# One weight tile for the state and output products of a chunked recurrence

## The chip, the cores and the metric

The kernel runs on one core of one Trainium2 chip. The metric is the device time of one execution in microseconds (us). A core has five engines with one instruction queue each: PE (TensorE, matrix products), DVE (VectorE), ACT (ScalarE), POOL (GpSimd) and SP (SyncE, which here only issues DMAs). Each engine takes its own instructions in order. In the profile PE's weight loads stand apart, as PEld.

## The reference, cut to what matters

The program is a trunk of two layers on 512 tokens of width 1024. The change touches the RWKV-7 branch of each layer:

```python
def rwkv7_scan(r, w, k, v, a, b):                    # 8 heads of 64 channels, 512 tokens
    def step(state, inp):
        r_t, w_t, k_t, v_t, a_t, b_t = inp
        sa = einsum('bhvk,bhk->bhv', state, a_t)
        state = state * w_t[:, :, None, :] + sa[..., None] * b_t[:, :, None, :] + v_t[..., None] * k_t[:, :, None, :]
        return state, einsum('bhvk,bhk->bhv', state, r_t)
    ...
# in rwkv7_branch, y is the scan's result, one head of 64 channels at a time:
    mean = jnp.mean(y, axis=-1, keepdims=True)
    var = jnp.mean(jnp.square(y - mean), axis=-1, keepdims=True)
    y = (y - mean) * lax.rsqrt(var + RWKV_LNX_EPS)
    ...
# in reference, for each layer:
        y_a, v_first = rwkv7_branch(cols_a, ...)     # then y_a @ w_branch_a
        y_b = dsa_branch(cols_b, ...)                # attention, then y_b @ w_branch_b
        merged = sigmoid(gate_a) * (y_a @ w_branch_a[l]) + sigmoid(gate_b) * (y_b @ w_branch_b[l])
        x = x + merged @ w_out[l]
```

After this come an attention into 256 memory tokens and a feed-forward part (dense in layer 0, eight experts in layer 1), which the change does not touch.

## The kernel before

**The recurrence in chunks.** The 512 tokens are cut into 8 chunks of 64, and the 8 heads into two groups `g` of 4. Within a group `jj` (0, 1) counts the pairs of heads and `e` (0, 1) the head of a pair; head `e` = 0 lives on partitions 0 to 63 and `e` = 1 on 64 to 127. What does not depend on the running state is worked out for all chunks at once: `rwkv_prep` makes decayed copies of the inputs, `rwkv_mats` the products of a chunk's tokens with each other, `rwkv_inverse` the inverse of a triangular matrix. `rwkv_chain` then walks the chunks. There are two layers with two groups each, so four such chains in the program.

**Operands of a chain.** `AM` holds for each head and chunk 192 columns on 128 partitions: columns 0 to 63 are a temporary, 64 to 127 weights for the output, 128 to 191 weights for the next state. `UV` holds the 128 x 64 matrix of the chunk's corrections and values. `art` holds 64 x 64 weights that multiply the incoming state `TT`: plane 0 for the next state and plane 1 for the output.

**A step of a chain.** For each of its four heads, a chunk makes two products for the next state, `AM[..., 128:192]` with `UV` (L885, weights 128 x 64) and `art` plane 0 with `TT` (L891, 64 x 64), added up in one PSUM bank `pS`. One DVE instruction (L893, 128 x 128) scales the sum of all four heads by the decay `WC` and writes the next chunk's `TT`. Two more products per head make the output, `AM[..., 64:128]` with `UV` (L900) and `art` plane 1 with `TT` (L906), in the banks `py0` and `py1`. The first chunk has no incoming state and the last makes no next one, which leaves 112 products in a chain. After four chunks, a half of the chain, `rwkv_center` takes each head's mean from the two banks (L919 the sums, L922 the subtraction) and writes `yc` to SBUF; after all eight, `rwkv_gn` normalises both halves (ACT L931 squares, DVE L932 and L934), turns them with four 128 x 128 transposes each (L938) and adds them to what the later steps use; `rwkv_out` (L951) multiplies by a gate and writes the pieces `yah` and `yal` for the branch's projection.

All these operands are 32-bit floats (f32). Each matrix product on f32 shows as two records on PE and two on PEld in the trace; a transpose shows as one.

**What runs beside it.** The branch and gate projections go through `proj_feat` (L285: f16 products of 128 x 128 weights with 512 columns). Its weights come from `wtile`: SP's queue loads the f32 tile `raw`, ACT converts it to `whi` (L263), DVE (L268) or, for every fourth tile, POOL (L266) makes the remainder `wlo`. The attention branch (L529, L546, L553) leaves its result in a DRAM buffer `ybd` (store L559), from which `branches` reads it back as `yb` (L1064) for the projections that run beside the second chain of a layer.

**What sets the order.** The program is written as generators, one for each branch, which `layer` advances in the turns of a written string (`ORDER`, L1633). A scheduler then orders the instructions of each engine by its own simulated timeline, so the order on an engine is not that of the code. The mixing stage of a layer has 8 PSUM banks: three in the pool `sm` (every tile that the recurrence names `pA`, `pB`, `paT`, `pG`, `pH`, `pMQ`, `pS`, `py0`, `py1`, `pyT`, `pg` takes one of these in turn), two for the attention, two for projections (`pf`) and one for `po`. The second group's inputs `sa`, `sr` and `bkb` wait in DRAM while the first group's chain runs: `rwkv_prep` stores them through SP's queue, and the loop that follows the first chain loads them into `art` and `bkb` again.

Of the kernel before, what the change touches and what calls it, by code (L numbers as in the profile page):

```python
# [19 lines left out]
P = 128  # L20
# [34 lines left out]
class Kern:  # L55
# [506 lines left out]
    def rwkv(self, l, cx, sx, hh, hl, ya):  # L562
# [60 lines left out]
        spill = [(self.dp.tile([P, 2, 8, 64], F32, name=f"spa{jj}", tag=f"spa{jj}", bufs=1),  # L623
# [74 lines left out]
    def rwkv_tiles(self, gp):  # L698

        t = lambda n, *s: gp.tile([P, *s], F32, name=n)  # L700
        return dict(AM=t("AM", 4, 8, 192), UV=t("UV", 8, 2, 2, 64), TT=t("TT", 2, 8, 64), TN=t("TN", 2, 8, 32),
                    art=t("art", 2, 2, 8, 64))

    def rwkv_prep(self, j, tp, q, art, spill=None):
# [49 lines left out]
        pa = art[:, 0] if spill is None else tp.tile([P, 8, 64], F32, name="sa", tag="tA")  # L754
        nc.vector.scalar_tensor_tensor(pa, ch(kr), -1.0, W[:, :, 0:64], OP.mult, OP.mult)
        pr = art[:, 1] if spill is None else tp.tile([P, 8, 64], F32, name="sr", tag="tB")
        nc.vector.tensor_tensor(pr, ch(r), W[:, :, 1:65], OP.mult)
        if spill is not None:
            nc.sync.dma_start(spill[:, 0], pa)
            nc.sync.dma_start(spill[:, 1], pr)  # L760
# [20 lines left out]
    def rwkv_mats(self, g, jj, q, G, bkb):  # L781


        nc, c = self.nc, self.c
        AM, UV, art = G["AM"], G["UV"], G["art"][:, jj]
        Xs = [slice(0, 64), slice(64, 128)]
        rmask = c["rmask"][:, None, :].to_broadcast([P, 4, P])
        for c4 in range(2):
            pA = [self.sm("pA") for _ in range(2)]
            for ci in range(4):  # L790
                for e in range(2):
                    nc.tensor.matmul(pA[e][:, ci * P:(ci + 1) * P], lhsT=bkb[Xs[e], c4 * 4 + ci].rearrange("p a b -> p (a b)"),
                                     rhs=art[Xs[e], :, c4 * 4 + ci, :], start=True, stop=True)
            for e in range(2):
                nc.vector.tensor_tensor(AM[:, 2 * jj + e, c4 * 4:c4 * 4 + 4, 0:P], pA[e].rearrange("p (c t) -> p c t", c=4),
                                        rmask, OP.mult)
        for e in range(2):
# [4 lines left out]
            nc.scalar.copy(AM[:, 2 * jj + e, :, P:192], pB.rearrange("p (c t) -> p c t", c=8))  # L802
        pa = self.sm("paT")
        for cc in range(8):
            for X in Xs:
                nc.tensor.matmul(pa[X, cc * 64:(cc + 1) * 64], lhsT=art[X, 0, cc, :], rhs=self.ident[X, X], start=True, stop=True)
        self.halves(UV[:, :, jj], pa)

# [23 lines left out]
    def rwkv_chain(self, g, tp, q, G):  # L832
# [25 lines left out]
        id2 = self.c["id2"][:, None, :].to_broadcast([P, 4, 64])  # L858
        for c4 in range(2):
            for jj in range(2):  # L860
# [6 lines left out]
                p4 = pq.rearrange("p (c x t) -> p c x t", c=4, x=2)  # L867
                cs = slice(c4 * 4, c4 * 4 + 4)
                nc.vector.tensor_tensor(art[:, jj, 0, cs, :], p4[:, :, 1, :], id2, OP.add)
                nc.vector.tensor_tensor(art[:, jj, 1, cs, :], p4[:, :, 0, :], art[:, jj, 1, cs, :], OP.add)  # L870

        ps = self.sm("pS")
        ys = []
        for cc in range(8):
            tt, T = cc // 2, slice((cc % 2) * 64, (cc % 2) * 64 + 64)
            if cc % 4 == 0:
                py = [self.sm("py0"), self.sm("py1")]
                first = {}
                fs = {}
            for jj in range(2):  # L880
                for e in range(2):
                    h, X = 2 * jj + e, Xs[e]
                    if cc < 7:
                        po = ps[X, (cc % 4) * P + jj * 64:(cc % 4) * P + jj * 64 + 64]
                        m = mm(po, lhsT=AM[:, h, cc, P:192], rhs=UV[:, cc, jj, e, :], start=e not in fs, stop=cc == 0,  # L885
                               skip_group_check=True)
                        if e in fs:
                            self.order(m.ins, fs[e])
                        fs.setdefault(e, m.ins)
                        if cc:  # L890
                            mm(po, lhsT=art[X, jj, 0, cc, :], rhs=TT[X, jj, cc, :], start=False, stop=True, skip_group_check=True)  # L891
            if cc < 7:
                nc.vector.tensor_tensor(TT[:, :, cc + 1, :], ps[:, (cc % 4) * P:(cc % 4 + 1) * P].rearrange("p (j t) -> p j t", j=2),  # L893
                                        WC[:, :, cc:cc + 1].to_broadcast([P, 2, 64]), OP.mult)
            for jj in range(2):
                for e in range(2):
                    h, X = 2 * jj + e, Xs[e]
                    yo = py[e][T, (tt % 2) * P + jj * 64:(tt % 2) * P + jj * 64 + 64]
                    k = e, cc % 2
                    m = mm(yo, lhsT=AM[:, h, cc, 64:P], rhs=UV[:, cc, jj, e, :], start=k not in first, stop=cc == 0,  # L900
                           skip_group_check=True)
                    if k in first:
                        self.order(m.ins, first[k])
                    first.setdefault(k, m.ins)
                    if cc:
                        mm(yo, lhsT=art[X, jj, 1, cc, :], rhs=TT[X, jj, cc, :], start=False, stop=True, skip_group_check=True)  # L906
            if cc % 4 == 3:
                ys.append(self.rwkv_center(tp, py, "tA" if cc < 4 else "tB"))
        for hf in range(2):
            self.rwkv_gn(tp, ys[hf], q, g, hf)  # L910

    def rwkv_center(self, tp, py, tag):

        nc = self.nc
        mean = tp.tile([P, 2, 4], F32, name="mean", bufs=2)
        yc = tp.tile([P, 4, 2, 64], F32, name="yc", tag=tag)
        pe = [p[:, 0:256].rearrange("p (a d) -> p a d", a=4) for p in py]
        for e in range(2):
# [836 lines left out]
```

## Time and profile before

| | |
|---|---|
| time, median of 3 runs | 2184.46 us (2177.66 to 2187.46) |
| profiled execution, its own time | 2181.56 us |
| its span, first to last instruction | 2179.8 us |
| mean granted TensorE clock | 0.962 |
| PE busy | 2038.4 us (94%), 16712 records |
| PEld busy | 1317.0 us (60%) |
| DVE busy | 1368.0 us (63%), 2326 instructions |
| ACT busy | 987.9 us (45%), 1545 instructions |
| POOL busy | 325.7 us (15%), 338 instructions |
| DMA | 332.48 MB, mean 153 GB/s |
| first chain of layer 0, its chunks on PE | about 283 to 338 us |
| second chain of layer 0 | about 477 to 524 us |
| first chain of layer 1 | about 1299 to 1359 us |
| second chain of layer 1 | about 1495 to 1551 us |

Busy times of different engines overlap, so only an engine with nothing to wait for in a stretch says what bounds that stretch. A row of a timeline gives start and length in us, engine, line, operation, the tiles (out<-in), how much of the array the weights take (partitions x columns), the shape of the moving operand, its type and the number of records; in brackets stand idle time before it and what ended that. Records on PE overlap in their lengths, so the cost of a run of records is read from the start of the first to the start of what follows.

### The profile page before, as it was taken

How to read it: one execution, taken by the hardware profiler on the slowest of the kernel's cores; microseconds unless marked ns; L12 is line 12 of the kernel's file. 1: busy time of each engine (PE TensorE's matmuls, PEld its weight loads, DVE VectorE, ACT ScalarE, POOL GpSimd, SP SyncE). 2: the span in 40 equal slices, each digit the busy share in tenths (PEclk: the TensorE clock that was granted, in tenths of full speed). 3: DMA queues.
4: the chain of work that ended last, by engine and by line, in shares of the span. 5: the costliest groups of instructions: out<-in, count | busy, mean ns of one | idle time of the engine just before them, and what ended most of it. 6: DMA issues, size and time to landing. Idle time of an engine off the chain costs nothing. (4 is left out here: it accounts for less than half of the span.)

```text
span 2179.8 us, 40496 instructions
## 1 busy us (share of the span) xinstructions
PE 2038.4 (94%) x16712; PEld 1317.0 (60%) x16712; DVE 1368.0 (63%) x2326; ACT 987.9 (45%) x1545; POOL 325.7 (15%) x338
## 2 busy tenths in 40 slices
PE   8998899898998999999999989999799799999997
PEld 4664455464464544444583555535355599999996
DVE  6767975644665433322567995463554688888886
ACT  5533334441353333321443443442233378887883
POOL 2351500002010000000251340001200120000002
PEclk9998999999998999999999999999899899999998
DMA  7342324342542333333334222334151799999993
GB/s 223 101 101 75 111 61 114 78 150 60 191 150 67 104 100 104 104 99 102 116 82 106 84 85 73 96 89 144 55 178 35 251 354 383 360 355 345 343 344 132
DMA packets 339538, 332.48 MB, mean 153 GB/s; under 512 B 93697, under 2 KB 255617, under 8 KB 339346
## 3 DMA queue, kind: packets, MB, share of 16 engines
q1 hardware_dynamic: 328240, 306.03, 44.2%
q10 hardware_dynamic: 8482, 15.39, 2.1%
q0 software_dynamic: 2624, 8.40, 1.1%
q8 instruction: 133, 2.18, 0.4%
q14 instruction: 59, 0.48, 0.1%
HBM read 297.05 MB, written 32.72 MB: 151 GB/s over the span
## 5 line engine op out<-in xcount | busy, mean ns | idle before, releaser
L263 ACT ACTIVATE whi<-raw 128x1024 f16<-128x1024 f32 (+3 forms) x242 | 226.9, 939 | 501.6 <-PE pf L285 278.0
L268 DVE SCALAR_TENSOR_TENSOR wlo<-raw,whi 128x1024 f16<-128x1024 f32 (+3 forms) x208 | 233.3, 1123 | 215.0 <-ACT whi L263 202.0
L1510 DVE SCALAR_TENSOR_TENSOR ewlo<-eraw,ewhi 128x1024 f16<-128x1024 f32 x265 | 320.2, 1219 | 57.7 <-ACT ewhi L1509 56.8
L285 PEld LDWEIGHTS <-whi 128*128 128x128 f16 x1888 | 183.6, 99 | 245.9 <-issue 48.0
L1509 ACT ACTIVATE ewhi<-eraw 128x1024 f16<-128x1024 f32 x265 | 276.6, 1053 | 77.7 <-PE py L1569 34.1
L1524 PE MATMUL pe<-XT,ewhi 128*128 128x144 f16 x2816 | 206.1, 226 | 0.5 <-issue 0.5
L1524 PEld LDWEIGHTS <-ewhi 128*128 128x128 f16 x2816 | 183.2, 98 | 1.2 <-issue 0.6
L285 PE MATMUL pf<-hh,whi 128*128 128x512 f16 x448 | 172.4, 385 | 5.0 <-ACT qe L481 2.6
L285 PE MATMUL pf<-hl,whi 128*128 128x512 f16 x448 | 172.0, 384 | 0.0
L285 PEld LDWEIGHTS <-wlo 128*128 128x128 f16 x944 | 92.0, 99 | 116.5 <-issue 15.9
L285 PE MATMUL pf<-fh,whi 128*128 128x512 f16 x336 | 127.3, 379 | 0.0
L285 PE MATMUL pf<-fl,whi 128*128 128x512 f16 x336 | 127.3, 379 | 0.0
L266 POOL TENSOR_TENSOR wlo<-raw,whi 128x1024 f16<-128x1024 f32 (+3 forms) x34 | 60.3, 1772 | 410.8 <-ACT raw L265 262.9
L1524 PE MATMUL pe<-XT,ewlo 128*128 128x144 f16 x1408 | 116.8, 226 | 0.1
L285 PE MATMUL pf<-hh,wlo 128*128 128x512 f16 x448 | 112.7, 385 | 0.0
L1569 PE MATMUL py<-HT,ewhi 128*128 128x144 f16 x1408 | 103.9, 227 | 0.1
L164 POOL TENSOR_TENSOR rs<-rs,nrm_e 128x1 f32<-128x1 f32 x28 | 16.7, 596 | 520.1 <-DVE rs L163 520.1
L1524 PEld LDWEIGHTS <-ewlo 128*128 128x128 f16 x1408 | 94.1, 98 | 0.3 <-DVE ewlo L1510 0.3
L1569 PEld LDWEIGHTS <-ewhi 128*128 128x128 f16 x1408 | 92.5, 98 | 0.3 <-issue 0.2
L285 PE MATMUL pf<-fh,wlo 128*128 128x512 f16 x336 | 79.4, 379 | 0.0
L345 PE MATMUL ptok<-whi,hh 128*128 128x256 f16 (+1 forms) x320 | 75.8, 276 | 0.0
L345 PE MATMUL ptok<-whi,hl 128*128 128x256 f16 (+1 forms) x320 | 75.5, 276 | 0.0
(437 smaller groups left out, 3886.0 us busy)
## 6 DMA issues: line engine op xcount, KB each, us to landing
raw<-in_w_in_dram SPq DMA_DIRECT2D x76, 512.0 KB
eraw<-in_moe_wg_dram SPq DMA_DIRECT2D x16, 2048.0 KB
eraw<-in_moe_wu_dram SPq DMA_DIRECT2D x16, 2048.0 KB
eraw<-in_moe_wd_dram SPq DMA_DIRECT2D x16, 2048.0 KB
eraw<-in_moe_wg_dram SPq DMA_DIRECT2D x8, 1536.0 KB
eraw<-in_moe_wu_dram SPq DMA_DIRECT2D x8, 1536.0 KB
eraw<-in_moe_wd_dram SPq DMA_DIRECT2D x8, 1536.0 KB
raw<-in_ffn_wg_dram SPq DMA_DIRECT2D x22, 512.0 KB
```

Of the source, the lines that this page charges most:

```text
L164: nc.gpsimd.tensor_tensor(out, out, self.nrm_e[:, :n], OP.pow)
L263: nc.scalar.activation(hi, raw, AF.Copy, scale=SW)
L266: nc.gpsimd.tensor_tensor(lo, raw, hi, OP.subtract)
L268: nc.vector.scalar_tensor_tensor(lo, raw, SW, hi, OP.mult, OP.subtract)
L285: self.nc.tensor.matmul(p, lhsT=w[:, k, :], rhs=x[k], start=first, stop=last)
L345: mm(p, lhsT=x[:, k0 + k, ts], rhs=w[:, k, :], start=k0 == 0 and t % 2 == 0 and first, stop=k0 + kg == kt and last, skip_group_check=True)
L1509: nc.scalar.activation(r[0], w, AF.Copy, scale=SW)
L1510: nc.vector.scalar_tensor_tensor(r[1], w, SW, r[0], OP.mult, OP.subtract)
L1524: mm(p[:, i * n:(i + 1) * n], lhsT=w[:, k, :], rhs=XT[:, k, h, :], start=z == 0, stop=z == len(ms) - 1)
L1569: mm(ps[d], lhsT=w[:, i, d * P:(d + 1) * P], rhs=HT[:, k, h, :], start=k == 0 and w is wh and h == 0 and d % per == 0, stop=k == FT - 1 an ...
```

## The change

Per head and chunk the two products with `AM` become one, and so do the two with `art`. `AM[:, h, cc, 64:192]` (128 columns of weights) with `UV` and `art[X, jj, cc]` (64 partitions x 128 columns) with `TT` each fill 128 partitions of PSUM: 64 of them the next state, 64 the output. For the state to land on the partitions of its head (`Xs[e]`, where `TT` lives), the two halves of the columns stand in one order for `e` = 0 and in the other for `e` = 1; the output lands on the opposite partitions `Ys[e]`. The sums of a head parity `e` go to a bank of their own, `pSy`, for four chunks.

With this go:

- `art` and its copy in DRAM are laid out as [partition, jj, chunk, plane, 64] in place of [partition, jj, plane, chunk, 64]; the stores of `sa` and `sr` to DRAM go to runs of 64 floats.
- `rwkv_mats` puts the columns of `AM` in the order of the parity, then writes an identity into the state's plane of `art`, so that one addition per half and `jj` updates both planes: one ACT copy (64 x 512) of the output's plane on partitions 64 to 127, and two POOL copies (64 x 512) of `id2`.
- `TT` of the next chunk is written by two DVE instructions of 64 x 128, one per parity.
- The outputs of a chunk go from PSUM to `yc` in SBUF by two ACT copies of 64 x 128, and `rwkv_center` works in place on `yc` with instructions of 128 x 512.
- `yc` now holds a token's rows by parity on opposite partitions, so the turn before the gate is 16 f32 products of 64 x 64 with the identity per half in place of four 128 x 128 transposes.

```diff
@@ rwkv, rwkv_tiles, rwkv_prep @@
-        spill = [(self.dp.tile([P, 2, 8, 64], F32, name=f"spa{jj}", tag=f"spa{jj}", bufs=1),
+        spill = [(self.dp.tile([P, 8, 2, 64], F32, name=f"spa{jj}", tag=f"spa{jj}", bufs=1),
-                    art=t("art", 2, 2, 8, 64))
+                    art=t("art", 2, 8, 2, 64))
-            nc.sync.dma_start(spill[:, 0], pa)
-            nc.sync.dma_start(spill[:, 1], pr)
+            nc.sync.dma_start(spill[:, :, 0, :], pa)
+            nc.sync.dma_start(spill[:, :, 1, :], pr)
@@ rwkv_mats @@
-                nc.vector.tensor_tensor(AM[:, 2 * jj + e, c4 * 4:c4 * 4 + 4, 0:P], pA[e].rearrange("p (c t) -> p c t", c=4),
-                                        rmask, OP.mult)
+                am = AM[:, 2 * jj + e, c4 * 4:c4 * 4 + 4, :].rearrange("p c (x t) -> p c x t", x=3)
+                nc.vector.tensor_tensor(am[:, :, 0:3 - e:2 - e, :], pA[e].rearrange("p (c x t) -> p c x t", c=4, x=2), rmask, OP.mult)
...
-            nc.scalar.copy(AM[:, 2 * jj + e, :, P:192], pB.rearrange("p (c t) -> p c t", c=8))
+            nc.scalar.copy(AM[:, 2 * jj + e, :, 64 + 64 * e:P + 64 * e], pB.rearrange("p (c t) -> p c t", c=8))
...
         self.halves(UV[:, :, jj], pa)
+
+        id2 = c["id2"][:, None, :].to_broadcast([P, 8, 64])
+        nc.scalar.copy(art[Xs[1], :, 0, :], art[Xs[1], :, 1, :])
+        for e in range(2):
+            nc.gpsimd.tensor_copy(art[Xs[e], :, e, :], id2[Xs[e]])
@@ rwkv_chain @@
-                nc.vector.tensor_tensor(art[:, jj, 0, cs, :], p4[:, :, 1, :], id2, OP.add)
-                nc.vector.tensor_tensor(art[:, jj, 1, cs, :], p4[:, :, 0, :], art[:, jj, 1, cs, :], OP.add)
-        (per chunk: L885, L891, L893, L900, L906, as printed above)
+                at = art[:, jj, c4 * 4:c4 * 4 + 4]
+                nc.vector.tensor_tensor(at, pq.rearrange("p (c x t) -> p c x t", c=4, x=2), at, OP.add)
+        yc = []
+        for cc in range(8):
+            if cc % 4 == 0:
+                yc.append(tp.tile([P, 8, 64], F32, name="yc", tag="tA" if cc < 4 else "tB"))
+                p = [self.sm("pSy").rearrange("p (c j d) -> p c j d", c=4, j=2) for _ in range(2)]
+                first = [None, None]
+            for x in range(2 if cc else 1):
+                for e in range(2):
+                    for jj in range(2):
+                        if x:
+                            l, r = art[Xs[e], jj, cc].rearrange("p x t -> p (x t)"), TT[Xs[e], jj, cc, :]
+                        else:
+                            l, r = AM[:, 2 * jj + e, cc, 64:192], UV[:, cc, jj, e, :]
+                        m = mm(p[e][:, cc % 4, jj, :], lhsT=l, rhs=r, start=first[e] is None, stop=x == (1 if cc else 0),
+                               skip_group_check=True)
...
+            for e in range(2):
+                if cc < 7:
+                    X = Xs[e]
+                    nc.vector.tensor_tensor(TT[X, :, cc + 1, :], p[e][X, cc % 4], WC[X, :, cc:cc + 1].to_broadcast([64, 2, 64]), OP.mult)
+            for e in range(2):
+                nc.scalar.copy(yc[-1][Ys[e], 2 * (cc % 4):2 * (cc % 4) + 2, :], p[e][Ys[e], cc % 4])
             if cc % 4 == 3:
-                ys.append(self.rwkv_center(tp, py, "tA" if cc < 4 else "tB"))
+                self.rwkv_center(tp, yc[-1])
@@ rwkv_center, rwkv_gn @@
+        nc.vector.tensor_reduce(mean, yc, AX.X, OP.add)
         nc.vector.tensor_scalar(mean, mean, 1.0 / 64, None, OP.mult)
+        nc.vector.tensor_tensor(yc, yc, mean[:, :, None].to_broadcast([P, 8, 64]), OP.subtract)
...
         for jj in range(2):
-            for t in range(2):
-                nc.tensor.transpose(pt[:, (2 * jj + t) * P:(2 * jj + t + 1) * P], yc[:, 2 * t + jj].rearrange("p e d -> p (e d)"),
-                                    self.ident)
+            for ci in range(4):
+                for X, Y in zip(Xs, Xs[::-1]):
+                    nc.tensor.matmul(pt[X, (4 * jj + ci) * 64:(4 * jj + ci + 1) * 64], lhsT=yc[Y, 2 * ci + jj, :], rhs=self.ident[Y, Y],
+                                     start=True, stop=True)
```

In the changed file the products of a chunk are at L889, the update of `TT` at L897, the ACT copy of the outputs at L899, the turn `pyT` at L927.

Three places of the instruction order follow, before and with the change; the number of an instruction in its queue is left out, and a tile's number is part of its name.

PE, second chain of layer 1, one chunk between two projections, before (`pf` is a projection, `py_12575` and `py_12576` are the two output banks):

```order
L285 MATMUL pf<-yb,wlo 128x512
L885 MATMUL pS<-UV,AM 64x64
L891 MATMUL pS<-TT,art 64x64
L885 MATMUL pS<-UV,AM 64x64
L891 MATMUL pS<-TT,art 64x64
...
L906 MATMUL py_12575<-TT,art 64x64
L906 MATMUL py_12576<-TT,art 64x64
L900 MATMUL py_12575<-UV,AM 64x64
L906 MATMUL py_12575<-TT,art 64x64
L900 MATMUL py_12576<-UV,AM 64x64
```

The same place with the change, the whole chunk:

```order
L285 MATMUL pf<-yb,wlo 128x512
L889 MATMUL pSy<-UV,AM 128x64 x2
L889 MATMUL pSy<-TT,art 128x64 x2
L889 MATMUL pSy<-UV,AM 128x64 x2
L889 MATMUL pSy<-TT,art 128x64 x2
L285 LDWEIGHTS whi
L285 MATMUL pf<-yb,whi 128x512
```

Sixteen products that mostly alternate between a weight tile of 128 x 64 and one of 64 x 64 became eight that come in pairs of one shape. Over the whole PE queue, neighbouring products whose weights take another number of partitions or columns of the array (these two counts rounded up to 64 or 128) are 781 before and 514 with the change; of these, 390 and 105 lie within or at the edges of the chunks' products.

PE, second chain of layer 0, its beginning, before (`po<-pT,vt` is the attention's last product):

```order
L865 MATMUL pMQ<-AM 64x128 x16
L553 MATMUL po<-pT,vt 64x256 x4
L865 MATMUL pMQ<-AM 64x128 x16
L885 MATMUL pS<-UV,AM 64x64 x4
L900 MATMUL py_4159<-UV,AM 64x64 x3
L900 MATMUL py_4160<-UV,AM 64x64 x3
...
L900 MATMUL py_4160<-UV,AM 64x64
L285 LDWEIGHTS whi
L285 MATMUL pf<-yb,whi 128x512
```

And with the change:

```order
L553 MATMUL po<-pT,vt 64x256 x4
L285 LDWEIGHTS whi
L285 MATMUL pf<-yah_2773,whi 128x512
...
L861 MATMUL pH<-H_3996,TT 64x64 x8
L861 MATMUL pH<-H_3997,TT 64x64 x8
L870 MATMUL pMQ<-AM 64x128 x32
L889 MATMUL pSy<-UV,AM 128x64 x2
L285 LDWEIGHTS whi
L285 MATMUL pf<-yb,whi 128x512
```

The first projection that reads `yb` stood behind the first two chunks of the chain and now stands behind half of the first chunk; six projections of `yah` have moved in ahead of it.

ACT, second chain of layer 1, before (`whi<-raw` is the conversion of a weight tile for `proj_feat`):

```order
L200 CAST ybh<-po 128x256
L263 ACTIVATE whi<-raw 128x512 x3
L265 ACTIVATE raw<-raw 128x512
L263 ACTIVATE whi<-raw 128x512 x2
L931 ACTIVATE ysq<-yc 128x512
L263 ACTIVATE whi<-raw 128x256 x2
```

And with the change:

```order
L899 COPY yc<-pSy 64x128 x3
L263 ACTIVATE whi<-raw 128x512
L899 COPY yc<-pSy 64x128
L263 ACTIVATE whi<-raw 128x512
L899 COPY yc<-pSy 64x128
L265 ACTIVATE raw<-raw 128x512
L263 ACTIVATE whi<-raw 128x512
L899 COPY yc<-pSy 64x128 x2
L263 ACTIVATE whi<-raw 128x512
L918 ACTIVATE ysq<-yc 128x512
```

Between the conversions of the weights, ACT's queue now holds the copies of the chunks' outputs.

More of the change, by code (lines that the diff above doesn't have):

```diff
@@ L786, in rwkv_mats @@
         Xs = [slice(0, 64), slice(64, 128)]
-        rmask = c["rmask"][:, None, :].to_broadcast([P, 4, P])
+        rmask = c["rmask"].rearrange("p (x t) -> p x t", x=2)[:, None, :, :].to_broadcast([P, 4, 2, 64])
         for c4 in range(2):
@@ L805, in rwkv_mats @@
             for X in Xs:
-                nc.tensor.matmul(pa[X, cc * 64:(cc + 1) * 64], lhsT=art[X, 0, cc, :], rhs=self.ident[X, X], start=True, stop=True)
+                nc.tensor.matmul(pa[X, cc * 64:(cc + 1) * 64], lhsT=art[X, cc, 0, :], rhs=self.ident[X, X], start=True, stop=True)
         self.halves(UV[:, :, jj], pa)
+        id2 = c["id2"][:, None, :].to_broadcast([P, 8, 64])
+        nc.scalar.copy(art[Xs[1], :, 0, :], art[Xs[1], :, 1, :])
+        for e in range(2):
+            nc.gpsimd.tensor_copy(art[Xs[e], :, e, :], id2[Xs[e]])
     def rwkv_values(self, g, jj, q, G):
@@ L857, in rwkv_chain @@
             self.halves(UV[:, :, jj], ph)
-        id2 = self.c["id2"][:, None, :].to_broadcast([P, 4, 64])
         for c4 in range(2):
@@ L881, in rwkv_chain @@
                 for e in range(2):
[L882 to L885, printed above, removed]
-                               skip_group_check=True)
[L887 to L906, printed above, removed]
+                    for jj in range(2):
[4 more added lines that the diff above has]
+                        m = mm(p[e][:, cc % 4, jj, :], lhsT=l, rhs=r, start=first[e] is None, stop=x == (1 if cc else 0),
+                               skip_group_check=True)
+                        if first[e] is not None:
+                            self.order(m.ins, first[e])
+                        first[e] = first[e] or m.ins
@@ L909, in rwkv_chain, with rwkv_center @@
         for hf in range(2):
-            self.rwkv_gn(tp, ys[hf], q, g, hf)
-    def rwkv_center(self, tp, py, tag):
+            self.rwkv_gn(tp, yc[hf], q, g, hf)
+    def rwkv_center(self, tp, yc):
         nc = self.nc
[L915 to L918, printed above, removed]
-            nc.vector.tensor_reduce(mean[:, e, :], pe[e], AX.X, OP.add)
+        mean = tp.tile([P, 8], F32, name="mean", bufs=2)
+        nc.vector.tensor_reduce(mean, yc, AX.X, OP.add)
@@ L920, in rwkv_center @@
         nc.vector.tensor_scalar(mean, mean, 1.0 / 64, None, OP.mult)
-        for e in range(2):
-            nc.vector.tensor_tensor(yc[:, :, e, :], pe[e], mean[:, e, :, None].to_broadcast([P, 4, 64]), OP.subtract)
-        return yc
+        nc.vector.tensor_tensor(yc, yc, mean[:, :, None].to_broadcast([P, 8, 64]), OP.subtract)
     def rwkv_gn(self, tp, yc, q, g, hf):
```

21 lines of the change are left out of this document (6 added, 15 removed).

## The prediction

> **What bounds the kernel now.** I read the page's head first, then the busy times of each engine in stretches of 20 us around the four chains, then the timeline of PE inside one chunk.
>
> ```profile
> span 2179.8 us, 40496 instructions
> PE 2038.4 (94%) x16712; PEld 1317.0 (60%) x16712; DVE 1368.0 (63%) x2326; ACT 987.9 (45%) x1545; POOL 325.7 (15%) x338
> ```
>
> The second view gives for each stretch its length and the busy time (and instructions) of PE, PEld, DVE, ACT and POOL, then the granted clock, the DMA share and GB/s:
>
> ```profile
> 300.00:320.00 20.00, 20.00 (x123) 11.61 (x124) 13.73 (x41) 7.49 (x17) 3.78 (x2) 1.00 0.16 47
> 320.00:340.00 20.00, 20.00 (x130) 11.54 (x129) 11.96 (x30) 6.53 (x17) 0.00 (x0) 1.00 0.33 86
> 500.00:520.00 20.00, 20.00 (x139) 12.07 (x138) 5.76 (x12) 2.31 (x4) 8.34 (x6) 1.00 0.25 73
> 520.00:540.00 20.00, 13.45 (x54) 6.26 (x53) 11.07 (x22) 3.84 (x8) 4.47 (x4) 0.83 0.13 41
> 1520.00:1540.00 20.00, 20.00 (x136) 11.85 (x134) 9.18 (x18) 2.31 (x4) 8.63 (x6) 1.00 0.25 73
> 1540.00:1560.00 20.00, 12.53 (x76) 7.25 (x74) 6.24 (x17) 2.13 (x5) 5.28 (x7) 0.76 0.08 15
> ```
>
> Where the chains run, PE is busy 20.00 us of 20 while DVE has 6 us or more to spare and ACT 12 or more. PE sets the end there, and what is taken off it comes off the end, until a chain ends (the stretches from 520 and 1540, where PE waits for the normalisation). One chunk of a chain:
>
> ```profile
> 1536.54 0.33 PE L885 MATMUL pS<-UV,AM 128*64 128x64 f32 x2
> 1536.79 0.33 PE L891 MATMUL pS<-TT,art 64*64 64x64 f32 x2
> 1537.05 0.33 PE L885 MATMUL pS<-UV,AM 128*64 128x64 f32 x2
> ...
> 1538.45 0.33 PE L906 MATMUL py<-TT,art 64*64 64x64 f32 x3
> 1538.71 0.33 PE L900 MATMUL py<-UV,AM 128*64 128x64 f32 x2
> ...
> 1540.11 0.57 PE L285 MATMUL pf<-yb,whi 128*128 128x512 f16 x1
> ```
>
> From 1536.54 to 1540.11 are 3.57 us for 16 products (32 records). A product between two of the other shape takes 0.25 to 0.26 from start to start. Is that the array's time, or the price of alternating? Rows in which one shape repeats answer:
>
> ```profile
> 97.26 1.15 PE L806 MATMUL paT<-ct,art 64*64 64x64 f32 x32
> 98.34 0.69 PE L715 MATMUL pz<-x,wa 64*128 64x512 f32 x1
> ```
>
> Thirty-two records of 64 x 64 took 1.08 us, 0.034 each, so the two records of a product are worth 0.07 and **a change of shape costs 0.256 - 0.07 = 0.19 us**; with 0.054 a record (below) it is 0.15. I take 0.17. The chunk has 14 such changes, 2.4 us: two thirds of its time is alternation.
>
> **The change part by part.**
>
> *Removed: the chunks' products.* Their groups:
>
> ```profile
> L885 PE MATMUL pS<-UV,AM 128*64 128x64 f32 x224 | 33.2, 244 | 0.0
> L891 PE MATMUL pS<-TT,art 64*64 64x64 f32 x192 | 31.2, 242 | 0.0
> L900 PE MATMUL py<-UV,AM 128*64 128x64 f32 x256 | 34.7, 245 | 0.3 <-DVE art L870 0.3
> L906 PE MATMUL py<-TT,art 64*64 64x64 f32 x224 | 30.5, 241 | 0.0
> ```
>
> 896 records at the chunk's 3.57/32 = 0.112 would be 100 us. Summed chunk by chunk from start to next start, the four chains take 24.0, 23.9, 24.7 and 24.8 us: **97.4 us**; the first chunk of each chain is of one shape and cheaper.
>
> *Added: products of 128 columns.* 240 of them, 480 records. The nearest rows for what such a record costs are products with full 128 x 128 f32 weights, first with 2 columns streamed, then with 256:
>
> ```profile
> 646.41 0.95 PE L1176 MATMUL pss<-ones,aq 128*128 128x2 f32 x8
> 647.23 0.38 PE L285 MATMUL pf<-qh,wlo 128*128 128x512 f16 x1
> ...
> 681.76 1.03 PE L1189 MATMUL pms<-akT,aqT 128*128 128x256 f32 x4
> 682.62 0.81 PE L327 MATMUL ptok<-whi,oh 128*128 128x512 f16 x3
> ```
>
> With almost nothing to stream, eight records took 0.82 us: 0.102 each, which is then the weight load. With 256 columns four took 0.86: 0.215 each, or 0.054 for each 64 columns, with no room for a load on top. So the load runs behind the products, and a record with 128 weight columns and 64 streamed costs the larger of the two, 0.102, against 0.156 if the load stood in series. I take 0.102: 480 x 0.102 = 49.0 us. Shape changes at or within the chunks fall from 390 to 105: 105 x 0.17 = 17.9 (15.8 to 20.0). The new chains thus cost 66.9, **a gain of 30.5 us** (28 to 33 by the price of a change).
>
> Against this stands a rule of the Trainium skill, "TensorE: Matmul & The Clock Gate", Part 3 on packing small matmuls: a weight load overlaps running products only when it goes to other rows of the array. By it the full-height loads would run in series, 0.156 a record, and the gain would be 97.4 - 74.9 - 17.9 = 4.6 us. The 0.215 of L1189, whose weights fill all rows, does not agree with it here.
>
> *Other shape changes* in the PE order grow by 18 (514 - 105 against 781 - 390): +3.1 us.
>
> *The turn.* The transposes, in a warm and in a cold place:
>
> ```profile
> 523.76 0.66 PE L938 MATMUL pyT<-ct,yc 128*128 128x128 f32 x4
> 524.25 0.38 PE L285 MATMUL pf<-yb,whi 128*128 128x512 f16 x1
> ...
> 1558.99 1.09 PE L938 MATMUL pyT<-ct,yc 128*128 128x128 f32 x4 [7.47 <-DVE yc L934]
> 1559.87 3.62 PE L951 MATMUL pg<-x,g 128*128 128x512 f32 x4
> ```
>
> Eight halves at 0.49 are 3.9 us now; 256 records of 64 x 64 at 0.034 are 8.7: +4.8. Behind the wait at 1558.99 the same four transposes took 0.88, 1.8 times as long; there the 32 records should take 2.0, which is counted with the tail.
>
> PE alone: -30.5 + 3.1 + 4.8 = -22.6.
>
> *DVE and ACT.*
>
> ```profile
> L893 DVE TENSOR_TENSOR TT<-pS,WC 128x128 f32<-128x128 f32 x28 | 8.1, 290 | 42.8 <-PE pS L891 42.8
> L869 DVE TENSOR_TENSOR art<-pMQ,ct 128x256 f32<-128x256 f32 x16 | 6.7, 418 | 2.4 <-PE pMQ L865 2.0
> L919 DVE TENSOR_REDUCE mean<-py 128x4 f32<-128x256 f32 x16 | 6.7, 424 | 6.3 <-PE py L906 5.7
> L922 DVE TENSOR_TENSOR yc<-py,mean 128x256 f32<-128x256 f32 x16 | 6.0, 418 | 0.1
> L409 ACT ACTIVATE vt<-ptok 128x128 f32<-128x128 f32 x4 | 1.1, 274 | 0.0
> L744 POOL COPY rnx<-rn 128x512 f32<-128x512 f32 x8 | 7.2, 903 | 0.3
> ```
>
> The update of `TT` splits in two of as many columns (56 x 0.29, +8.1 us of DVE); `art` and the centring do the same columns in half the instructions, nothing or a little less. Hidden: DVE has 6 to 14 us free in each 20. A chunk's answer comes 0.29 later, behind projections; without that cover it is 28 x 0.29 = 8 us. ACT gets 64 copies near 0.27 (17.5 us, 12 of 20 free): hidden too if they don't block (rival below).
>
> *The tails.* After the last chunk centring is no longer 2 x 0.424 + 2 x 0.418 = 1.7 but two copies, then at most 0.85 + 0.84: +0.5 in each layer. The turn adds 1.1 cold in layer 1 and about 0.5 in layer 0 beyond its warm cost: +2 together.
>
> *`rwkv_mats`.* The identity fills are two POOL copies near 0.9 and an ACT copy of some 0.6 for each of eight calls; POOL works 3.8 us or less in the stretches from 300 and 320. They free `art` later for `pMQ`, long after. Zero, or all of them in the open 8 x 0.25 to 8 x 0.5 = 2 to 4; I take +2.
>
> *The store of `sa` and `sr` in short runs* goes through SP's queue:
>
> ```profile
> 255.31 0.34 SPq L760 DMA_DIRECT2D spa<-sr  x1
> ...
> L660 SPq DMA_DIRECT2D art<-spa x4: 332/382/425, 338.4 to 1359.3; - x4
> ```
>
> It is issued at 255 and read back from 338 on: 83 us of cover. Nothing, if the other loads of SP's queue don't notice 2048 more packets among 339538.
>
> *The read-back of `yb`.* The new order moves the first projection that reads it:
>
> ```profile
> 482.77 1.02 PE L285 MATMUL pf<-yb,whi 128*128 128x512 f16 x4 [0.36 <-DMA yb<-ybd]
> ...
> 1499.28 1.01 PE L285 MATMUL pf<-yb,whi 128*128 128x512 f16 x2 [2.90 <-DMA yb<-ybd]
> ```
>
> In layer 0 two chunks stood between the attention's last product and this reader; now there are six projections (1.3 us), the products of `pH` and `pMQ`, and half a chunk: about 2 to 2.5 us less cover, where 0.36 was already uncovered. +2. In layer 1 it waited anyway: 0.
>
> **Sum:** -22.6 + 2 (tails) + 2 (`rwkv_mats`) + 2 (`yb`) = -16.6 us against the profiled 2181.56, which is 2.9 below the median shown. 2165.0 from the one, 2167.9 from the other; I say **2165**.
>
> **The rivals.**
>
> *More is saved* (10%). Products of 64 rows from the two heads could run side by side, as the 0.034 of L806 suggests (below its 0.054 for streaming 64 columns): 224 records at 0.05 in place of 0.102 take another 11 us, and uncovered terms of 4 drop: about 2150. Against it: in the new order two products of one head stand together, on the same rows.
>
> *The supply takes half back* (16%). PE's projections now come sooner, and their weights must too. ACT shows the slack:
>
> ```profile
> 1521.52 0.63 ACT L263 ACTIVATE whi<-raw 128x512 f16<-128x512 f32 x1 [4.82 <-PE pf L285]
> ```
>
> It waits for PE to give back a buffer, so the supply is ahead in the second chains; in the first ones DVE, at 13.73 of 20, is nearer to a bound. If DVE's 8 us came out in the open: 2173.
>
> *The load is in series* (10%), for a reason that L1189 does not show: 480 x 0.156 + 17.9 = 92.8, so the chains gain only 4.6, and 3.1 + 4.8 + 6 are added: 2181.6 + 9.3 = 2191. This is what the skill's rule above comes to (the Trainium skill, the same page and part).
>
> *ACT's queue becomes the wait* (13%, the slower side). The copies `yc<-pSy` wait for a chunk's last product, and behind them in the queue stand the conversions of weights (0.63 each) that the projections between chunks need; before, nothing in ACT's queue there waited for the chain save `ysq`. A blocked conversion is late by itself and the remainder `wlo`, about 1.3 us for a chunk; 28 chunks make 36 us: 2181.6 - 16.6 + 36 = 2201. It decides for a loss from 13 such chunks. Against: the same 4.82 of waiting, more than a conversion and a copy, and up to three buffers of weights ahead.
>
> **Chances.** Forecast 51% (2155 to 2175 by itself), the rivals as given. Half a per cent, 11 us, is about what can be told from no change: faster is below 2173.5. The forecast gives nine tenths of its chance there, the first rival all, the supply half: 0.66. The same: the rest of these two, most of the series load, a little of ACT's queue: 0.21. Slower 0.13. The range leaves out the ends of both rivals: 2147 to 2189.
>
> **What would show it.** Right: a full chunk of eight products near 2.3 us on PE from start to start, records of L889 0.10 apart where a shape repeats; PE's busy time 20 us or so lower; PE still at 20.00 in the stretches of the chains, which end earlier; no idle time of PE before L285 put down to ACT's `whi`. Wrong: records of L889 near 0.16 apart; PE idle before L285 with ACT's L899 ahead of it; PE waiting for DVE's L897 between chunks; a wait for `yb` in layer 0 well above 2.4.

## The result, and the profile after

The changed kernel takes 2149.95 us (median of 4 runs, 2147.86 to 2151.00); the kernel before, on the same chip, 2181.06 (2174.54 to 2187.46). The ratio is 0.9847, with a 95% interval of 0.9811 to 0.9883: **about 31 to 33 us faster, twice the 16.6 that the prediction's sum gave.** The range held it; the size did not hold. Timed again on another occasion the ratio was 0.9864 (0.9818 to 0.9909).

The head of the page of the changed kernel's profiled execution (2149.16 us):

```profile
span 2147.3 us, 40225 instructions
PE 2006.6 (93%) x16520; PEld 1310.3 (61%) x16520; DVE 1379.4 (64%) x2322; ACT 1011.8 (47%) x1617; POOL 334.8 (16%) x354
```

PE's busy time fell by 31.8 us and the span by 32.5. The gain came off PE almost one for one, so PE was the bound in the main, as the prediction read it. The chains now run at about 299 to 346, 476 to 515, 1304 to 1353 and 1481 to 1518 us. Stretches in and around them, with the columns of the prediction's table:

```profile
300.00:320.00 20.00, 20.00 (x114) 12.74 (x112) 19.15 (x58) 10.98 (x29) 2.14 (x1) 1.00 0.25 72
320.00:340.00 20.00, 20.00 (x133) 12.87 (x131) 7.73 (x24) 8.95 (x24) 1.65 (x1) 1.00 0.24 64
500.00:520.00 20.00, 15.13 (x121) 10.77 (x118) 11.83 (x23) 4.59 (x13) 8.29 (x6) 0.91 0.21 66
1300.00:1320.00 20.00, 16.35 (x95) 10.60 (x95) 19.50 (x53) 4.79 (x14) 0.00 (x0) 0.83 0.03 9
1480.00:1500.00 20.00, 20.00 (x129) 13.34 (x124) 8.62 (x18) 5.13 (x13) 7.32 (x5) 1.00 0.65 210
1500.00:1520.00 20.00, 18.38 (x135) 12.36 (x133) 11.71 (x26) 4.90 (x14) 8.43 (x9) 0.99 0.21 54
```

In most of them PE is still full until a chain ends (515 and 1518 us). The beginnings of the two first chains are the exception: there DVE is nearly full now (19.15 and 19.50 of 20), and from 1300 to 1320 PE is no longer. Before the change that stretch was

```profile
1300.00:1320.00 20.00, 20.00 (x115) 10.79 (x113) 12.55 (x34) 4.90 (x12) 0.00 (x0) 0.83 0.15 41
```

and PE waited nowhere within the two first chains. With the change it waits at their beginnings for DVE's update of `art` and for ACT's copies:

```profile
299.16 0.66 PE L889 MATMUL pSy<-UV,AM 128*128 128x64 f32 x4 [2.40 <-DVE art L873]
...
1300.69 3.34 PE L870 MATMUL pMQ<-AM 64*64 64x128 f32 x32 [2.65 <-ACT UV L836]
...
1307.90 0.66 PE L889 MATMUL pSy<-UV,AM 128*128 128x64 f32 x4 [1.16 <-DVE art L873]
...
1314.32 0.66 PE L889 MATMUL pSy<-UV,AM 128*128 128x64 f32 x4 [1.49 <-ACT yc L899]
```

In the whole trace these waits come to 3.6 us for `art`, 2.7 for `UV` and 1.8 for `yc`; before, PE waited 0.3 for `art` at these products and nothing for the others.

A full chunk in the second chain of layer 1:

```profile
1496.43 0.55 PE L889 MATMUL pSy<-UV,AM 128*128 128x64 f32 x4
1496.92 0.66 PE L889 MATMUL pSy<-TT,art 64*128 64x64 f32 x4
1497.50 0.66 PE L889 MATMUL pSy<-UV,AM 128*128 128x64 f32 x4
1498.09 0.66 PE L889 MATMUL pSy<-TT,art 64*128 64x64 f32 x4
1498.68 1.90 PE L285 MATMUL pf<-yb,whi 128*128 128x512 f16 x8
```

From 1496.43 to 1498.68 are 2.25 us, where the old chunk took 3.57 and the prediction expected 2.3. Each pair of products (4 records) takes 0.58 to 0.59 behind a change of shape, and 0.49 behind a projection, whose weights have the same 128 x 128. Summed from start to next start, by the names of the tiles, the four chains take 62.2 us; the old ones come to 98.3 in this way (97.4 in the prediction's sum by lines). This sum is used for all kernels below.

Not every chunk has that order. In 8 of the 28 chunks with both kinds of product, all four products of TT with art stand together, two on partitions 0 to 63 and two on 64 to 127:

```profile
1339.64 1.00 PE L889 MATMUL pSy<-UV,AM 128*128 128x64 f32 x8
1340.57 0.67 PE L889 MATMUL pSy<-TT,art 64*128 64x64 f32 x8
1341.17 1.15 PE L927 MATMUL pyT<-ct,yc 64*64 64x64 f32 x32
```

Eight records then take 0.60, no more than four of one head (0.59).

The turn and the tails, and the read-back of `yb`, by the timeline and by the view of waits:

```profile
521.33 1.98 PE L927 MATMUL pyT<-ct,yc 64*64 64x64 f32 x32 [6.19 <-DVE yc L921]
523.23 3.57 PE L940 MATMUL pg<-x,g 128*128 128x512 f32 x4
...
1524.60 1.97 PE L927 MATMUL pyT<-ct,yc 64*64 64x64 f32 x32 [6.22 <-DVE yc L921]
1526.50 3.70 PE L940 MATMUL pg<-x,g 128*128 128x512 f32 x4
```

```profile
477.60 0.59 PE L285 MATMUL pf<-yb,whi 128*128 128x512 f16 x2 [0.87 <-DMA yb<-ybd]
...
480.54 1.67 PE L285 MATMUL pf<-yb,whi 128*128 128x512 f16 x7 [1.96 <-DMA yb<-ybd]
...
1478.30 0.59 PE L285 MATMUL pf<-yb,whi 128*128 128x512 f16 x2 [1.89 <-DMA yb<-ybd]
```

The 32 records of a half's turn (16 products) take 1.90 us behind a wait, against 0.88 for the four transposes; the wait ahead of them is 6.2 in both layers, where it was 5.8 and 7.5. `yb` is now waited for in layer 0, 0.87 + 1.96 where it was 0.36, and less in layer 1, 1.89 where the first wait alone was 2.90.

### The profile page after: what moved, and what is told of

It is laid out like the page before. It is cut to its first block, busy times and chain, and to the rows that moved or that the text cites. A ratio compares the mean times of both kernels' runs of the same rounds, so it can differ in the third digit from the quotient of the medians.

```text
span 2147.3 us, 40225 instructions
## 1 busy us (share of the span) xinstructions
PE 2006.6 (93%) x16520; PEld 1310.3 (61%) x16520; DVE 1379.4 (64%) x2322; ACT 1011.8 (47%) x1617; POOL 334.8 (16%) x354
## 2 busy tenths in 40 slices
DMA packets 346706, 332.47 MB, mean 155 GB/s; under 512 B 101889, under 2 KB 263809, under 8 KB 346514
## 4 chain that ended last, share of the span: by engine, by line
PE 70%; DVE 15%; DMA 5%; issue 3%; ACT 2%; SPq 2%; POOL 1%; another core or an unknown queue 0%; ACTq 0%; DVEq 0%; POOLq 0%
PE pf L285 20%; PE pe L1513 12%; PE ptok L327 10%; PE py L1558 6%; PE ptok L345 3%; PE pf L297 3%; PE pSy L889 3%; DVE iacc L514 2%; DVE m L513 2%; DVE wlo L268 2%; PE po L553 1%; PE psc L529 1%; PE pl L503 1%; DVE pr L988 1%; PE pA L793 1%
## 5 line engine op out<-in xcount | busy, mean ns | idle before, releaser
L285 PEld LDWEIGHTS <-wlo 128*128 128x128 f16 x944 | 92.9, 100 | 113.0 <-issue 12.4
```

Source lines behind the costliest of these rows:

```text
L285: self.nc.tensor.matmul(p, lhsT=w[:, k, :], rhs=x[k], start=first, stop=last)
```

## The experiments

The prediction's model has three prices: 0.034 us for a record with 64 columns of weights, 0.10 for one with 128, and 0.17 for a change of the weights' shape. If they are right, most of the gain has nothing to do with fusing products: it is the ordering that fusing brought along. The rival is that products cost their time in any order and the gain is their number, 448 to 240. The runs take the two apart. The table has each kernel's result; "chains" is PE's time in the chunks' products from start to next start without idle time, "changes" the changes of shape at or within them and in the whole PE order, "clock" the mean granted TensorE clock of the profiled execution, and "lost" is (1 - clock) x span.

| kernel | median us | ratio to before (95%) | products | changes | chains us | clock | lost us |
|---|---|---|---|---|---|---|---|
| before | 2181.06 | | 448 | 390 / 781 | 98.3 | 0.962 | 83 |
| changed | 2149.95 | 0.9847 (0.9811 to 0.9883) | 240 | 105 / 514 | 62.2 | 0.960 | 86 |
| changed, again | 2149.18 | 0.9864 (0.9818 to 0.9909) | 240 | 105 / 514 | 63.6 | 0.958 | 90 |
| 64 columns, grouped | 2099.61 | 0.9616 (0.9569 to 0.9662) | 448 | 118 / 506 | 45.7 | 0.967 | 69 |
| the same, outputs first | 2106.92 | 0.9669 (0.9623 to 0.9716) | 448 | 124 / 530 | 45.8 | 0.970 | 63 |
| changed, alternating | 2185.72 | 1.0025 (0.9998 to 1.0052) | 240 | 231 / 628 | 87.2 | 0.953 | 103 |
| only UV with AM fused | 2144.38 | 0.9848 (0.9805 to 0.9891) | 352 | 68 / 449 | 45.4 | 0.955 | 96 |
| changed, grouped | 2152.00 | 0.9832 (0.9793 to 0.9871) | 240 | 76 / 461 | 53.7 | 0.949 | 110 |
| the same, rows alternate | 2148.12 | 0.9840 (0.9800 to 0.9881) | 240 | 73 / 452 | 54.1 | 0.957 | 92 |
| all copies doubled | 2167.01 | 0.9919 (0.9890 to 0.9949) | 240 | 118 / 515 | 70.5 | 0.957 | 93 |
| fills doubled | 2152.30 | 0.9877 (0.9841 to 0.9914) | 240 | 127 / 531 | 71.9 | 0.963 | 79 |
| copies on DVE | 2149.34 | 0.9869 (0.9816 to 0.9921) | 240 | 118 / 514 | 67.1 | 0.961 | 84 |

**The changed kernel again.**

> The changed kernel once more, on the chip of the three runs beside it, as what they are compared with. Between 2148 and 2155 us, some 30 us below the kernel before.

2149.18 us. It is what the three runs after it are held against.

**The old products, in another order.** In the code nothing but the order within a chunk differs from the kernel before (the scheduler orders the rest anew around it); `self.order` ties one instruction behind another on PE.

```diff
-        (per head: state UV, state TT; then per head: output UV, output TT)
+            for x in range(2):                       # state, output
+                for jj in range(2):
+                    for e in range(2):
+                        m = mm(out(jj, e) if x else state(jj, Xs[e]), lhsT=AM[:, h, cc, 64:P] if x else AM[:, h, cc, P:192],
+                               rhs=UV[:, cc, jj, e, :], ...)
+                        uv.append(m.ins)
+            for x in range(2):                       # then all of TT with art
+                ...
+                        m = mm(..., lhsT=art[Xs[e], jj, x, cc, :], rhs=TT[Xs[e], jj, cc, :], ...)
+                        for w in uv:
+                            self.order(m.ins, w)
```

(In chunk 4, where the output banks change, state and output are two groups.)

> The kernel before with its 448 products of 64 weight columns left as they are, but ordered within a chunk: first all products of UV with AM (128x64), then all of TT with art (64x64). Shape changes at or within the chunks fall from 390 to 118. Theory (the price is the change of shape, 0.17 us each): the chunks cost 480 records x 0.048 + 416 x 0.034 + 118 x 0.17 = 57 us in place of 98, so the kernel gets as fast as the changed one or faster: about 2140, with no fused product in it. Rival (a product costs its 0.22 us of array time in any order, and only their number counts): no gain, within 5 us of the kernel before.

2099.61 us: 81 us below the kernel before and 50 below the changed one, with all 448 products and no fused one. The rival is dead. A chunk of it on PE:

```profile
1448.90 0.45 PE L905 MATMUL pS<-UV,AM 128*64 128x64 f32 x8
1449.28 0.38 PE L889 MATMUL pS<-TT,art 64*64 64x64 f32 x5
...
1449.56 0.40 PE L889 MATMUL py<-TT,art 64*64 64x64 f32 x7
1449.88 0.68 PE L905 MATMUL py<-UV,AM 128*64 128x64 f32 x8
1450.40 1.89 PE L553 MATMUL po<-pT,vt 128*64 128x256 f32 x8
```

Sixteen products, 32 records, in 1.50 us (1448.90 to 1450.40) where the old order took 3.57 and the fused products take 2.25. The eight products of TT with art (16 records) fit in 0.60, their change of shape included; the prediction's 0.034 a record was, if anything, too much. The chains come to 45.7 us, not the 57 expected: four products of UV with AM take 0.38, and I had priced their records at 0.048 by such a row of before, which held a change too, so that the sum counted those changes twice.

The kernel gained 74.8 us of span, the chains 52.6. Of the other 22, PE's idle time takes 12.6: the second chain of layer 1 ends while projections are left to cover its tail, and the wait before the turn falls from 13.3 us in all to 3.3. The rest, some 9 us, was not traced by itself; the clock's account below differs by 14.

**The fused products, alternating.**

```diff
-            for x in range(2 if cc else 1):
-                for e in range(2):
-                    for jj in range(2):
+            for e in range(2):
+                for jj in range(2):
+                    for x in range(2 if cc else 1):
+                        ...
+                        if last is not None: self.order(m.ins, last)
```

> The changed kernel with its 240 products forced to alternate, UV with AM then TT with art for each head: shape changes at or within the chunks go from 105 to 231. Theory (0.17 us for each change): +126 x 0.17 = 21 us, about 2170. Rival (the number of products and their 0.097 us for a record set the time): within 4 us of the changed kernel.

```profile
1522.16 0.33 PE L890 MATMUL pSy<-UV,AM 128*128 128x64 f32 x2
1522.42 0.43 PE L890 MATMUL pSy<-TT,art 64*128 64x64 f32 x2
1522.78 0.43 PE L890 MATMUL pSy<-UV,AM 128*128 128x64 f32 x2
1523.14 0.43 PE L890 MATMUL pSy<-TT,art 64*128 64x64 f32 x2
1523.51 0.39 PE L285 MATMUL pf<-yb,whi 128*128 128x512 f16 x1
```

2185.72 us: with 240 fused products in the wrong order the whole gain is gone. The first product, behind a projection of its own shape, takes 0.26; each that follows a change takes 0.36. Two records at 0.097 are 0.19, so the change costs 0.17, the prediction's price. By the chains (87.2 against 63.6 with 126 changes more) it is 0.19. The chains explain 24 of the 37 us; the clock's account is 13 higher, which would be the others (an estimate, (1 - clock) x span).

**One product fused, the other not.** UV with AM as in the change, TT with art as two products of 64 x 64 into the same bank, all of UV ahead of all of TT, the rows of the two heads alternating.

```diff
-                            l, r = art[Xs[e], jj, cc].rearrange("p x t -> p (x t)"), TT[Xs[e], jj, cc, :]
+            for x in range(2 if cc else 0):
+                for jj in range(2):
+                    for e in range(2):
+                        m = mm(p[e][(Xs, Ys)[x][e], cc % 4, jj, :], lhsT=art[Xs[e], jj, cc, (e + x) % 2, :],
+                               rhs=TT[Xs[e], jj, cc, :], start=False, stop=True, skip_group_check=True)
```

> The changed kernel with only the product of UV with AM fused (128 columns of weights); TT with art is split again in two products of 64x64, and within a chunk all of UV stand ahead of all of TT. Theory (records of 64x64 cost 0.034 each, those of 64x128 cost 0.097; a change of shape costs 0.17): 448 x 0.034 in place of 224 x 0.097 is -6.5, and 68 changes in place of 105 are -6.3, so 10 to 15 us below the changed kernel, about 2137. Rival (fewer products is what pays): 112 products more at 0.1 to 0.2 us, 11 to 22 us above the changed kernel.

```profile
1496.89 1.00 PE L887 MATMUL pSy<-UV,AM 128*128 128x64 f32 x8
1497.82 0.47 PE L896 MATMUL pSy<-TT,art 64*64 64x64 f32 x16
1498.23 0.39 PE L285 MATMUL pf<-yb,wlo 128*128 128x512 f16 x1
```

Eight products of 64 x 64 took 0.41 us, with the change back to 128 x 128 within it. The chains fell by 18 us to 45.4, more than expected, with 112 products more. The whole kernel came down by only 5 (2144.38 against 2149.18), which the spread of the runs (2140.37 to 2154.29) doesn't tell from nothing, and not by the 10 to 15 expected: PE's idle time grew by 13 us, 8 of them in the triangular inverse, and the granted clock was lower, 0.955. The rival, 11 to 22 us slower, did not happen.

**The fused products, grouped, in two orders of their rows.**

```diff
+                        if x and cc != 4:
+                            for w in uv: self.order(m.ins, w)      # TT behind all of UV
+                        elif not x:
+                            uv.append(m.ins)
```

and in the second of them `jj` outside and `e` inside, the products of TT of the second `jj` each tied behind the product before it.

> The changed kernel with its order alone altered: within a chunk all four products of UV with AM (128x128), then all four of TT with art (64x128), two of one head's rows and two of the other's. Shape changes at or within the chunks fall from 105 to 76, in the whole PE order from 514 to 461. Theory (a change of shape costs 0.19 us, the slope between the changed kernel and its alternating form): 53 x 0.19 = 10 us, about 2140, and the chunks near 58 us on PE in place of 63. Rival (all is in the count of products): within 3 us of 2150.

> As the run before it, but the four products of TT with art alternate between the rows of the two heads (0 to 63, 64 to 127). If products on different rows run side by side (the prediction's first rival, and the rule that a load overlaps products on other rows only), a record of these drops from 0.097 to about 0.05: 224 x 0.047 = 10 us less than the run before it, about 2130. If each record costs its load in any case, within 3 us of the run before it.

The first, then the second:

```profile
1501.28 1.00 PE L890 MATMUL pSy<-UV,AM 128*128 128x64 f32 x8
1502.21 0.67 PE L890 MATMUL pSy<-TT,art 64*128 64x64 f32 x8
1502.81 0.60 PE L285 MATMUL pf<-yb,whi 128*128 128x512 f16 x2
```

```profile
1499.41 1.00 PE L890 MATMUL pSy<-UV,AM 128*128 128x64 f32 x8
1500.35 0.66 PE L890 MATMUL pSy<-TT,art 64*128 64x64 f32 x8
1500.94 0.60 PE L285 MATMUL pf<-yb,wlo 128*128 128x512 f16 x2
```

Here stands a surprise. Eight records of TT with art take 0.60 us, as long as the four records of one head in the changed kernel (0.59). Two products on rows 0 to 63 and two on rows 64 to 127, next to each other, run side by side, in both orders of the code, as they do in 8 chunks of the changed kernel. So neither expectation for the second run was right as put: the overlap is real, and the first run had it already. The chains fell by 9.9 and 9.5 us, to 54 where 58 was expected, but the kernels did not follow: 2152.00 and 2148.12, no difference from 2149 that can be told. Their granted clock was 0.949 and 0.957.

**The copies.**

```diff
-                nc.scalar.copy(yc[-1][Ys[e], ...], p[e][Ys[e], cc % 4])
+                for _ in range(2):
+                    nc.scalar.copy(yc[-1][Ys[e], ...], p[e][Ys[e], cc % 4])
```

and the three fills of `art` in `rwkv_mats` likewise; then the fills alone; then, in place of that, `nc.vector.tensor_copy` for the copies of the outputs.

> The changed kernel with each added copy made twice: the 64 copies yc<-pSy on ACT (17 us of ACT), and the identity fills of art in rwkv_mats, 8 on ACT (5 us) and 16 on POOL (14 us). Theory (all of them lie beside PE): within 4 us of 2150, as the prediction's zero end has it. Rivals: the fills cost what the prediction took, +2 us, or up to 4; or ACT's queue is the wait, with 0.26 for each of 64 copies and the conversions behind them: +17 us or more.

> The changed kernel with only the identity fills of art in rwkv_mats made twice (8 ACT copies and 16 POOL copies more). Theory (they lie beside PE; what the run with all copies doubled lost came from the order that the scheduler built, above all from the waits for TN in the inverse): no instruction on PE waits for them, and the time is 2150 plus or minus 10, by what the new order happens to cover. Rival (the fills cost time themselves): +2 to +4 us with idle time of PE that names art on POOL or ACT.

> The changed kernel with the 64 copies of a chunk's outputs on DVE in place of ACT (17 us more on DVE, 17 less on ACT). If ACT's queue were a wait in the changed kernel, this would be 5 us or more faster and the conversions of weights would stand earlier. Theory (ACT has 12 of 20 us free there): within 10 us of 2150, without idle time of PE moving off ACT's whi; DVE's own work may push the scaling of the state later.

All doubled: 2167.01 us, 17 above the changed kernel, just what the rival of ACT's queue asked for. But the waits of PE say something else. The longest of that kernel's list and its wait for ACT's conversions, then the same two rows in the changed kernel's second trace (us in total, times, longest):

```profile
PE pY L1016 <- DMA TN<-scrN: 20.7, 11, 7.7
...
PE ptok L327 <- ACT whi L263: 4.7, 3, 1.9
```

```profile
PE pY L1013 <- DMA TN<-scrN: 4.2, 3, 2.5
PE ptok L327 <- ACT whi L263: 4.1, 3, 1.6
```

PE hardly waited longer for ACT's conversions (4.7 against 4.1). It waited 16 us more for the inverse's blocks to come back from DRAM, a round trip that other products on PE cover in the changed kernel's order; the scheduler, given other instructions, built an order that leaves it bare. Other waits fell, so that PE's idle time as a whole grew by 12.6, and the chains took 7 more, with 13 changes of shape more. That doubling the copies brought this on by way of the order, and not by holding something up, was not shown by itself. With the fills alone doubled the median is 2152.30, 2 to 3 us up, which the spread of the runs doesn't tell from nothing; no wait of PE there names `art` on POOL or ACT, as the rival asked. The copies moved from ACT to DVE change nothing that can be told (2149.34): PE then waits 2.6 us for them, where it waited 1.8 and 0 in the two traces of the changed kernel for ACT's. So the copies on ACT cost the changed kernel 1.8 us at most.

**The best order once more.** The grouped kernel with 64 columns, with the output's products of UV first (`for x in ((1, 0) if cc != 4 else (0, 1))`, and the state's tied behind them where a bank doesn't change).

> The grouped kernel with 64-column products once more with another order inside the group: the output's products of UV with AM ahead of the state's. 124 shape changes at or within the chunks in place of 118. Theory (grouping is what pays, not one lucky order): chunks within 3 us of the 46 that they took on PE, total 2090 to 2120. Rival (the grouped kernel's 2100 was half luck of the order): 2130 or more, with the chunks still near 46.

2106.92 us, chains 45.8. It is the grouping that pays, and not one lucky order. Its rival, 2130 or more, did not happen. PE's idle time is that of before here (130.3 us against 131.3), so of the 76 us by which its span is shorter, the chains explain 52.5 and idle time 1; the clock's account, 63 us against 83, would be most of the rest.

## Why the prediction was right or wrong

Term by term, the prediction against the two traces (2181.56 and 2149.16 us):

| term | predicted | measured |
|---|---|---|
| chunks' products | -30.5 | -36.1 (-34.7 in the second trace) |
| the turn | +4.8 | +5.6 |
| other PE work (other shape changes), what is left of the span | +3.1 | -0.8 |
| tails, `yb`, `rwkv_mats` (idle time of PE) | +6 | -1.2 |
| sum | -16.6 | -32.5 (the span) |

- **What bounds the kernel: right in the main.** What PE lost in busy time, the span lost. That DVE's work stays hidden was wrong at the beginnings of the two first chains, where PE now waits for `art`, `UV` and `yc`, 8.1 us in all (4.8 in the second trace); the prediction put this at nothing. Waits elsewhere fell by as much, so that it doesn't show in the sum.
- **The price of a change of shape, 0.17: right**, and measured apart: 0.17 by single products of the alternating kernel (0.14 with the 0.112 a record of the next point), 0.19 by its chains. The chunk at 2.3 us came out at 2.25. That most of the old chunk was alternation is shown by the old products in another order, 1.50 in place of 3.57.
- **The chunks' gain of 30.5 was 4 to 6 us too small**: the products took 62 to 64 us and not 66.9. Most of this is the side-by-side run of the two heads in the chunks whose TT products stand together: 8 chunks with eight records and 3 with six, some 4 us (an estimate: 38 records at 0.097 to 0.112). The price of a record was about right: four took 0.39 between two projections, 0.097 each, and 4, 8 and 12 records of UV with AM, each with the change behind them, took 0.48, 0.93 and 1.38, 0.112 for each further one, against 0.102. The load is hidden: had it stood in series, a pair would have taken 0.62 before any change of shape. So the rival of 0.156 a record falls. The Trainium skill's rule ("TensorE: Matmul & The Clock Gate", Part 3 on packing small matmuls), that a load overlaps only products on other rows, does not agree with the 0.097 to 0.112 of full-height weights; that products on other rows do overlap agrees with the 0.60 for eight records.
- **The step that failed is the sum of the small costs.** I took +3.1, +2, +2 and +2, all of one sign, for things that the profile did not show; together they came to about -2. That is 11 of the 16 us by which the sum was off; the chunks are the rest. The fills: no wait names them, and doubling them cost nothing that can be told. The other shape changes: not seen, PE's other work fell by 0.8. The tails: the cold turn, the one behind a wait, cost its 1.9 as predicted, but the waits ahead of the two turns fell from 13.3 to 12.4 in all. `yb`: +2.5 in layer 0, where +2 was predicted, and the reverse in layer 1, where I took 0, so that the total went from 5.1 to 4.7. Here some of these terms hid and some turned round; I let each one count, though the old order too had its share of bare waits (`psc` and `pb` waited 4.7 and 6.0 us for DVE, 0 and 1.7 with the change). Which edit took those away was not tried.
- **The rivals.** "More is saved" named the right time, 2150, and in part the right reason: products of two heads do run side by side, but in 11 chunks and not in all, which saved some 4 us and not 11; in most chunks a head's pair stands alone and takes 0.59. The small costs fell away by 11 us and not by 4. That the two misses add up to its 2150 is luck. The supply did not take half back, though DVE's 19.50 of 20 from 1300 us on is its sign. The copies in ACT's queue held PE up for 1.8 us at most.
- **Two slips that change nothing.** The chances for "faster" add up to 0.64 (nine tenths of 0.51, then 0.10 and 0.08), not 0.66. The short runs of `sa` and `sr` raised the packets from 339538 to 346706, by 7168 and not 2048; no wait of PE names them.
- **What I didn't ask.** My own prices said that two products of 64 columns on 64 rows (four records at 0.034) are cheaper than one of 128 (two at 0.10), and that 2.4 of 3.57 us were alternation. So the order was to be changed, not the products: that gives 81 us, 53 of them in the chains. Of the 18 us by which the changed kernel's chains (63.6) lie above those 45.7, 10 are its order (53.7 when grouped) and 8 the fused products; the turn costs 5.6 more.

## What to carry to other kernels

Before making small products larger, look at whether neighbours have the same shape of weights: here a change cost about 0.17 us, five records' worth at 0.034, and putting equal shapes together gained 81 us with the same products, 53 of them in these products' own time. A list of small costs that no row of the profile shows should not be added up with one sign: each is a bound, some are hidden, and a rebuilt order moves waits both ways. When an order is rebuilt, compare PE's time in the part that was changed, its idle time and its granted clock apart, for the whole time mixes the three.

## What was not expected of the hardware

Products with 64 x 64 weights were cheaper than the prediction's 0.034 a record: sixteen records in 0.41 us with a change within it, under 0.026 each. That is less than half of the 0.054 that streaming 64 columns takes by the prediction's L1189, so products on different quarters of the array run at the same time; with 0.17 taken off for the change it is 0.015, so more than three of the four at once (an estimate). Two products on different rows with 128 columns of weights did so too (0.60 for eight records, 0.59 for four).

The granted clock differs between orders of the same work. The view of cores, for the old products grouped and the fused products grouped:

```profile
core 0: 2105.0 us, clock 0.967
```

```profile
core 0: 2158.0 us, clock 0.949
```

If all of the span followed the clock, the same work at full clock would be some 69 us shorter in the first and 110 in the second (an estimate): 41 us between two kernels that differ by 8 us in their chains. Both profiled runs are the slowest of their kernel. Over the runs that were timed, the clock was 0.967 to 0.975 for the first, 0.948 to 0.958 for the second and 0.953 to 0.968 for the kernel before. With (1 - clock) x span taken off, the spans of all kernels in the table stand within 9 us of where the chains put them (the turn's 5.6 us not counted): against the kernel before, the grouped fused kernel is 49 us lower (chains -45), the one with only UV fused 52 (chains -53), the changed one 36 (chains -36), the grouped old products 61 (chains -53). That may be why 10 us less in the chains could be lost. The stretches below full clock lie mostly at or just behind idle time of PE (in the prediction's table of stretches, 0.83 and 0.76 where PE was busy 13.45 and 12.53 of 20), so an idle PE seems to be paid for twice. But not all do: before the change the clock was 0.83 from 1300 to 1320 us too, with PE busy 20.00. That idle time is the cause was not tried, and stays open.
